# Five hand-overs of a streaming-encoder layer: output weights, residual sums, one split, the order of FFN up's last products, and places and order of FFN down's first tiles

## The chip, the cores and the metric

The kernel runs on one core of one Trainium2 chip. The metric is the device time of one execution in microseconds (us), less is better. The engines are named as the profile names them: PE multiplies matrices (PEld is its weight load), DVE, ACT and POOL do elementwise work, SP issues most of the DMA transfers. Three runs of the kernel before are given, and one execution of it with a profile.

## What is computed

One layer of a streaming encoder over 1024 tokens of width 1024, in float32. Cut to what matters here:

```
mod = silu(c) @ ada_w + ada_b                       # six vectors: sh1, sc1, g1, sh2, sc2, g2
h = rmsnorm(x, ln1_g) * (1 + sc1) + sh1
q, k, v, cb, cc, cx, ga, gb = split(h @ w_in)
y_a = stick_breaking_attention(rmsnorm(q), rmsnorm(k), v)
y_b = cb * causal_dwconv(cc * cx, conv_w)
merged = sigmoid(ga) * (y_a @ w_branch_a) + sigmoid(gb) * (y_b @ w_branch_b)
x = x + g1 * (merged @ w_out)
h = rmsnorm(x, ln2_g) * (1 + sc2) + sh2
f = (silu(h @ w_ffn_gate) * (h @ w_ffn_up)) @ w_ffn_down      # hidden width 2816
x = x + g2 * f
```

## The kernel before

**Products.** Each float32 operand is split into a high part, which is a copy rounded to the PE's type (`whi`, `rh`), and a low part, the rest (`wlo`, `rl`). A product of two operands is three matmuls: high by high, high by low, low by high (L131 to L133, in `half_prod`; L1596 to L1598 in FFN down). A `split` makes the two parts of 512 columns of weights: ACT copies (`whi`, L1227), and DVE subtracts (`wlo`, L1228). So a weight goes from DMA to ACT to DVE to PE, and PE can take `whi` one step earlier than `wlo`.

**Stages and their times on the time axis of the profile.** Input projection and attention run to about 968 us. The branch projection (loop at L1174) multiplies by `w_a` and merges the branches, up to 1068. The output projection (loops at L1311) goes over two halves `ch` of the 1024 output columns, and within a half over eight token tiles `i`; it ends at 1163. FFN gate and up (`strassen`, loop over `j` = 0 to 10 at L1520) run to 1586, FFN down (`down`) to 1803. In a program with one instruction list per engine, each engine works through its own list in order; a scheduler orders the lists when the kernel is built, from the order of the code, and `tc.issue_after(x)` holds what is issued under it behind `x`. A tile with `bufs=1` has one buffer: whoever writes it next waits until the last reader is done.

**Output weights.** `preload_wo` (L1145) loads five blocks of 512 columns of `w_o` in three DMAs (`raw`, two of 1024 columns and one of 512) and splits them. It is called from the `w_a` loop two rows of `m` before the loop's end (L1175), ahead of the load of that row's `w_a`. Its three loads share one buffer of their own pool `wpx`.

**Residual sums.** After each tile's product `ps`, DVE multiplies it by `g1b` into `tm` (L1356, one buffer) and adds the residual `xi`. In the first half of the columns the sum goes into `tm` and is stored to `d_x1` (L1358, L1359); in the second half it goes into the right half of `x1` (L1363, two buffers), whose left half is loaded back. From `x1` ACT makes `xn` (L1373), the normed tile, which PE transposes later (`tail_tr`, L1251) into `h2b`, FFN's input.

**FFN gate and up.** `strassen` computes 2 x 2 blocks of columns and tokens with seven products instead of eight. The factors made of token blocks are `rh[q]`, `rl[q]` (q = 0 to 6), those made of weight blocks are sums `s1` to `s4` that are split when they are used. The products lie in PSUM banks, which the trace names `e`. The end of one call is, in order: p1 takes another product onto itself (`prod(p1, split(s1), 4, True)`); ACT copies p1 into `c12`; PE computes p3; DVE adds p7 to the copy (`c22`); then p7 takes a product onto itself. The program lines say this order; the scheduler may put PE's products in another one. `hidden` multiplies up by gate for each of the four results, and `put_f` stores seven tiles f (high and low part, 128 x 1024) to `d_f[q, j]`; for the last `j` the stores go through POOL's queue. For j = 0 the products are written out by hand ahead of the loop (L1393 to L1447): `split_big` makes `rh[4]`, `rl[4]` from the input, `up2 = split(ws1[1])` splits a sum of weights.

**FFN down.** `down` runs seven products q in the order 0, 1, 2, 5, 4, 6, 3, each over 11 blocks j of the hidden width and four token tiles; 12 matmuls per block and 132 per product. The weights `w_d` lie in four buffers `wd` that held FFN's inputs and in six more (`wdx`); the stored f tiles come back through a ring of six buffers, with f `q`,`j` loaded by `get_f`. All of this is allocated in the pool `phe2`, which takes the place of the pools of FFN up (`phe`, with `rh6`, `rl6`, `rh3`, `rl3`): a tile there waits for the last reader of what lay at the same place. The allocation order before:

```
u2t = [e2.tile([P, 512], F32, name=f"u2t{t}") for t in range(4)]
vt = [e2.tile([P, 512], F32, name=f"vt{t}") for t in range(4)]
f0 = e2.tile([P, 2, 512], F32R, tag="f", bufs=6, name=nm("f"))
```

SP issues, per block, the load of the weights and then the load of f (L1582 to L1585), so the first f stands behind those weight loads whose place comes free late.

## Time and profile before

| What | Value |
| --- | --- |
| three runs | 1808.14, 1805.36, 1806.92 us |
| their median | 1806.92 us |
| the profiled execution | 1806.53 us, of which the span from the first to the last instruction is 1804.5 |
| mean granted clock of PE | 0.997 of full speed |
| DMA | 359.07 MB, 199 GB/s over the span |

Each profile row below has the start in the span (us), the duration (us), the engine (SPq and POOLq are the queues that issue DMAs), the program line, the operation, the result and the operands with their shape. Brackets at the end give the idle time of the engine just before the row, and who ended it. The names are the program's, without buffer numbers; several buffers share one name. A row of the waits view has the engine, the tile and the line that waited, after the arrow who ended the wait, and then the waits' total, their number and the longest, in us. A row of the windows view has the stretch (from and to, us from the span's start), its length, the busy times of PE, PEld, DVE, ACT and POOL with their counts of instructions, then PE's granted clock, the busy share of the DMA engines, and GB/s. A row of the DMA view ends with the median time from issue to landing, or is headed by its least, median and most.

Matmuls overlap, so that a row's duration is longer than the distance to the next one's start; the distance is what counts for the time.

### The profile page before, as it was taken

The page shows a single profiled execution, that of the slowest core. Times are in us where ns is not written, and L with a number is a line of the kernel's source. Part 1 is how long each engine was busy: PE and PEld are TensorE (multiplying, and loading weights), DVE is VectorE, ACT ScalarE, POOL GpSimd, SP SyncE. Part 2 cuts the span into 40 slices and gives each one's busy share as a digit, 9 for nine tenths or more (in the row PEclk, how much of TensorE's full clock was granted, in tenths as well). Part 3 has the DMA queues.
Part 4 walks back from the last instruction along what each step waited for, and adds up shares of the span by engine and source line. Part 5 has one row for each costly group of instructions (what it writes and reads, how often), then busy time and mean ns, then how long its engine had stood idle before and what let it go on. Part 6 is the DMA issues. An engine that isn't in the chain of part 4 may idle for free.

```text
span 1804.5 us, 24915 instructions
## 1 busy us (share of the span) xinstructions
PE 1785.0 (99%) x8599; PEld 1486.4 (82%) x8599; DVE 1271.7 (70%) x2030; ACT 829.8 (46%) x1553; POOL 343.0 (19%) x437
## 2 busy tenths in 40 slices
PE   8999999999999999999999999999999999999999
PEld 6888877888888888888888888888888888878887
DVE  6876586777774678777785764698777777544776
ACT  5534364333433567766675221764544454432321
POOL 0024334723231333333341100100000000000000
PEclk9999999999999999999999999999999999999999
DMA  9569654223644967796655856425534344389776
GB/s 377 165 239 383 237 186 141 88 94 101 224 137 155 289 187 197 218 321 169 165 141 191 281 193 200 139 94 181 192 129 162 139 178 163 129 325 319 276 232 223
DMA packets 165009, 359.07 MB, mean 199 GB/s; under 512 B 15538, under 2 KB 60938, under 8 KB 163732
## 3 DMA queue, kind: packets, MB, share of 16 engines
q1 hardware_dynamic: 128300, 289.65, 48.9%
q10 hardware_dynamic: 33096, 55.25, 8.5%
q0 software_dynamic: 3488, 12.59, 2.0%
q8 instruction: 68, 1.11, 0.3%
q14 instruction: 57, 0.47, 0.1%
HBM read 247.84 MB, written 109.62 MB: 198 GB/s over the span
## 4 chain that ended last, share of the span: by engine, by line
PE 88%; DMA 4%; DVE 3%; ACT 2%; issue 1%; POOL 1%; ACTq 0%; SPq 0%; DVEq 0%; POOLq 0%
PE pj L293 9%; PE e L133 7%; PE e L131 7%; PE e L132 7%; PE pj L133 6%; PE pj L131 6%; PE pj L132 6%; PE pj L1018 4%; PE pj L1020 4%; PE pj L1019 4%; PE e L1596 4%; PE e L1598 4%; PE e L1597 4%; PE tr L942 3%; PE o L958 2%; PE z L913 2%
## 5 line engine op out<-in xcount | busy, mean ns | idle before, releaser
L1227 ACT ACTIVATE whi<-raw 128x512 fp32r<-128x512 f32 x137 | 84.9, 628 | 159.9 <-PE e L132 99.9
L136 POOL TENSOR_TENSOR pt<-pt 128x63 f32<-128x63 f32 (+7 forms) x128 | 101.8, 795 | 212.0 <-DVE pt L928 195.7
L1228 DVE TENSOR_TENSOR wlo<-raw,whi 128x512 fp32r<-128x512 f32 x137 | 93.2, 687 | 67.3 <-ACT whi L1227 49.8
L293 PE MATMUL pj<-whi,big 128*128 128x512 f32 x448 | 133.7, 396 | 3.8 <-ACT big L262 3.8
L132 PE MATMUL e<-big,whi 128*128 128x512 f32 x352 | 137.0, 389 | 0.0
L133 PE MATMUL e<-big,wlo 128*128 128x512 f32 x352 | 136.3, 389 | 0.6 <-DVE wlo L1228 0.6
L131 PE MATMUL e<-big,whi 128*128 128x512 f32 x352 | 136.5, 390 | 0.0
L946 DVE TENSOR_TENSOR atl<-tr,ath 128x512 fp32r<-128x512 f32 (+1 forms) x192 | 104.1, 553 | 34.2 <-ACT ath L945 32.9
L136 DVE TENSOR_TENSOR c<-pj,c 128x512 f32<-128x512 f32 x140 | 93.5, 683 | 47.3 <-PE pj L133 46.8
L131 PE MATMUL pj<-big,whi 128*128 128x512 f32 x320 | 125.0, 391 | 0.0
L133 PE MATMUL pj<-big,wlo 128*128 128x512 f32 x320 | 124.8, 390 | 0.0
L1596 PE MATMUL e<-whi,f 128*128 128x512 f32 (+1 forms) x319 | 122.5, 384 | 2.3 <-DMA f<-d_f 2.3
L132 PE MATMUL pj<-big,whi 128*128 128x512 f32 x320 | 124.6, 389 | 0.0
L1597 PE MATMUL e<-wlo,f 128*128 128x512 f32 (+1 forms) x319 | 122.3, 384 | 0.0
L1598 PE MATMUL e<-whi,f 128*128 128x512 f32 (+1 forms) x319 | 122.3, 384 | 0.0
L915 ACT ACTIVATE pt<-z,rq 128x128 f32<-128x128 f32 (+1 forms) x192 | 107.3, 579 | 26.7 <-PE z L914 23.7
L1018 PE MATMUL pj<-big,whi 128*128 128x512 f32 x256 | 113.2, 442 | 0.0
L136 DVE TENSOR_TENSOR wlo<-raw,whi 128x512 fp32r<-128x512 f32 x108 | 88.6, 824 | 29.8 <-ACT whi L516 29.6
L945 ACT ACTIVATE ath<-tr 128x512 fp32r<-128x512 f32 (+1 forms) x192 | 93.3, 488 | 28.7 <-PE tr L942 27.5
L131 PE MATMUL e<-rh,whi 128*128 128x512 f32 x264 | 102.8, 389 | 1.4 <-DVE c L136 1.4
L293 PEld LDWEIGHTS pj<-whi,big 128*128 128x128 f32 x448 | 84.8, 190 | 22.3 <-ACT big L262 4.6
L132 PE MATMUL e<-rl,whi 128*128 128x512 f32 x264 | 102.7, 389 | 0.0
(300 smaller groups left out, 4736.7 us busy)
## 6 DMA issues: line engine op xcount, KB each, us to landing
f<-d_f SPq DMA_DIRECT2D x77, 512.0 KB, 4.7
d_f<-fs SPq DMA_DIRECT2D x70, 512.0 KB, 3.2
raw<-w_cg SPq DMA_DIRECT2D x40, 512.0 KB, 3.6
raw<-w_u SPq DMA_DIRECT2D x26, 512.0 KB, 4.3
raw<-w_g SPq DMA_DIRECT2D x25, 512.0 KB, 4.0
raw<-w_kv SPq DMA_DIRECT2D x20, 512.0 KB, 5.0
ld<-ada SPq DMA_DIRECT2D x16, 512.0 KB, 6.8
d_t<-ts SPq DMA_DIRECT2D x16, 512.0 KB, 6.5
```

What stands on the lines that cost most here:

```text
L131: nc.tensor.matmul(ps, wh[:, k, :], fh[:, k, :], start=(k == 0 and not onto), stop=False, skip_group_check=onto)
L132: nc.tensor.matmul(ps, wh[:, k, :], fl[:, k, :], start=False, stop=False, skip_group_check=onto)
L133: nc.tensor.matmul(ps, wl[:, k, :], fh[:, k, :], start=False, stop=(k == 3), skip_group_check=onto)
L136: eng.tensor_tensor(out=out, in0=a, in1=b, op=op)
L293: nc.tensor.matmul(ps, a, b, start=(k == 0 and q == 0), stop=(k == KT - 1 and q == 2))
L915: nc.scalar.activation(pt[:, off + s0:off + s0 + m], z[:, :m], AF.Sigmoid, scale=rq[:, 1, i, h:h + 1])
L945: nc.scalar.activation(th[:, :nb, c0:c0 + P], src, AF.Copy)
L946: nc.vector.tensor_tensor(out=tl[:, :nb, c0:c0 + P], in0=src, in1=th[:, :nb, c0:c0 + P].bitcast(F32), op=ALU.subtract)
L1018: nc.tensor.matmul(ps, wh, rh_, start=(k == 0), stop=False)
L1596: nc.tensor.matmul(o, sh, w[0][:, c], start=(j == 0), stop=False)
L1597: nc.tensor.matmul(o, sh, w[1][:, c], start=False, stop=False)
L1598: nc.tensor.matmul(o, sl, w[0][:, c], start=False, stop=(j == NJ - 1))
```

## The change

Five places are edited.

- **Output weights:** `preload_wo` is called one row of `m` later, and after that row's load of `w_a`. Its first two loads use the ring `raw` of the weight pool `gw`, the third has a tile of 512 columns of its own in `wpx`.
- **Residual sums:** in the second half of the columns the product with `g1b` goes directly into `x1`, and the residual is added there; `tm` is used in the first half only.
- **One split:** `up2 = split(ws1[1])` stands ahead of the `split_big` of `rh[4]`.
- **FFN up's last products:** in the last call (j = 10, up) p3 is held behind the last matmul of the product onto p1. For this `prod` and `half_prod` return that matmul.
- **FFN down's first tiles:** the six f buffers have a name each, and are allocated as f4, f5, then two of the `wdx`, then f0 to f3; `rh3`, `rl3` are now allocated before `rh6`, `rl6`. The loads of f 0 to f 6 stand before those of the weights, and the weight loads from the ninth on are held behind the load of f 1.

```diff
@@ half_prod, prod
-            nc.tensor.matmul(ps, wl[:, k, :], fh[:, k, :], start=False, stop=(k == 3), skip_group_check=onto)
+            last = nc.tensor.matmul(ps, wl[:, k, :], fh[:, k, :], start=False, stop=(k == 3), skip_group_check=onto)
+        return last
...
-        half_prod(ps, w, rh[q], rl[q], onto)
+        return half_prod(ps, w, rh[q], rl[q], onto)
@@ preload_wo
-            raw = wx.tile([P, 1024], F32, tag="raw", bufs=1, name=nm("raw"))
+            raw = wx.tile([P, 512], F32, name=nm("raw")) if j == 2 else gw.tile([P, 1024], F32, tag="raw", bufs=GR, name=nm("raw"))
@@ the w_a loop
+        if n == 0:
+            wa[m] = load_ch(w_a[m])
+        if (m, n) == (KT - 1, 0):
             with tc.issue_after(last_m.ins):
                 preload_wo()
-        if n == 0:
-            wa[m] = load_ch(w_a[m])
@@ residual sums
-            tm = dp.tile([P, 512], F32, tag="tm", bufs=1, name=nm("tm"))
-            nc.vector.tensor_tensor(out=tm, in0=ps, in1=g1b[:, cs], op=ALU.mult)
             if ch == 0:
+                tm = dp.tile([P, 512], F32, tag="tm", bufs=1, name=nm("tm"))
+                nc.vector.tensor_tensor(out=tm, in0=ps, in1=g1b[:, cs], op=ALU.mult)
...
-            nc.vector.tensor_tensor(out=x1[:, cs], in0=tm, in1=xi, op=ALU.add)
+            nc.vector.tensor_tensor(out=x1[:, cs], in0=ps, in1=g1b[:, cs], op=ALU.mult)
+            nc.vector.tensor_tensor(out=x1[:, cs], in0=x1[:, cs], in1=xi, op=ALU.add)
@@ ahead of the FFN loop
-    for q in (6, 3):
+    for q in (3, 6):
         rh[q] = ep.tile([P, 4, 512], F32R, name=f"rh{q}")
         rl[q] = ep.tile([P, 4, 512], F32R, name=f"rl{q}")
...
+    up2 = split(ws1[1])
     split_big(rh[4], rl[4], h2b[0][1])
-    up2 = split(ws1[1])
@@ strassen
-            prod(p1, split(s1), 4, True)
+            last5 = prod(p1, split(s1), 4, True)
...
-        p3 = product(sp_4 or split(s4), 2)
+        with tc.issue_after(last5.ins) if (j, e) == (NJ - 1, 1) else ExitStack():
+            p3 = product(sp_4 or split(s4), 2)
@@ ahead of down
-    f0 = e2.tile([P, 2, 512], F32R, tag="f", bufs=6, name=nm("f"))
+
+    def f_tile(n):
+        return e2.tile([P, 2, 512], F32R, tag=f"f{n % 6}", bufs=1, name=nm("f"))
+
+    fring = {n: f_tile(n) for n in (4, 5)}
+    wdx = [e2.tile([P, 1024], F32, name=nm("wdx")) for n in range(2)]
+    fring.update((n, f_tile(n)) for n in range(4))
+    nf = itertools.count()
     wd = [bigp.tile([P, 4, 1024], F32, tag="big", bufs=4, name=nm("wd")) for n in range(4)]
-    wd = [w_[:, n, :] for w_ in wd for n in range(4)] + [e2.tile([P, 1024], F32, name=nm("wdx")) for n in range(2 * NJ - 16)]
+    wd = [w_[:, n, :] for w_ in wd for n in range(4)] + wdx
+    wd += [e2.tile([P, 1024], F32, name=nm("wdx")) for n in range(2 * NJ - 18)]
+
     def get_f(q, j):
-        f = e2.tile([P, 2, 512], F32R, tag="f", bufs=6, name=nm("f")) if (q, j) != (0, 0) else f0
+        n = next(nf)
+        f = fring.pop(n) if n in fring else f_tile(n)
...
+    for ht in range(7):
+        ftiles[0, ht] = get_f(0, ht)
+        if ht == 1:
+            f1_ld = last_f[0]
     for ht in range(NJ):
-        load_wd(ht, 0)
-        if ht < 7:
-            ftiles[0, ht] = get_f(0, ht)
+        with tc.issue_after(f1_ld.ins) if ht > 7 else ExitStack():
+            load_wd(ht, 0)
```

How the change moves instructions shows at three places. The rows give the line, the operation and the tiles with the numbers that the build gave them; the waits name what an instruction waits for (DMAHW, DMASW: transfers that were issued by hardware or software queues; PE, Activation, DVE, Pool: instructions of these engines), and what an engine has waited for already is not waited for again.

**SP at the start of FFN down, before.** `wd` is a buffer of four weight blocks, `f_15660` is f 0, `f_15674` f 1.

```order
L1580 DMA wd_15662<-w_d 128x512 [waits DMAHW1_49,PE_49]
L1580 DMA wd_15662<-w_d 128x512 [waits DMAHW2_49]
L1580 DMA wd_15662<-w_d 128x512 [waits DMAHW3_49]
L1580 DMA wd_15662<-w_d 128x512 [waits DMAHW4_49]
L1580 DMA wd_15663<-w_d 128x512 [waits DMAHW5_49,PE_49]
L1580 DMA wd_15663<-w_d 128x512 [waits DMAHW6_49]
L1580 DMA wd_15663<-w_d 128x512 [waits DMAHW7_49]
L1571 DMA f_15660<-d_f_0_12410 128x1024 [waits DMAHW0_49]
L1571 DMA f_15674<-d_f_1_12411 128x1024 [waits DMAHW1_49,PE_49]
L1571 DMA f_15677<-d_f_2_12412 128x1024 [waits DMAHW2_49,Pool_49]
```

The same place after the change, where `f_15656` is f 0, and `f_15652` and `f_15653` are f 4 and f 5; `wd_15661` is the buffer that was `wd_15662`.

```order
L1594 DMA wd_15661<-w_d 128x512 [waits DMAHW4_49]
L1585 DMA f_15656<-d_f_0_12402 128x1024 [waits DMAHW5_49,PE_49,Pool_49]
L1585 DMA f_15657<-d_f_1_12403 128x1024 [waits DMAHW6_49]
L1585 DMA f_15658<-d_f_2_12404 128x1024 [waits DMAHW7_49]
L1585 DMA f_15659<-d_f_3_12405 128x1024 [waits DMAHW0_49,Pool_49]
L1585 DMA f_15652<-d_f_4_12406 128x1024 [waits DMAHW1_49,PE_49]
L1585 DMA f_15653<-d_f_5_12407 128x1024 [waits DMAHW2_49]
L1594 DMA wd_15662<-w_d 128x512 [waits DMAHW3_49]
L1594 DMA wd_15662<-w_d 128x512 [waits DMAHW4_49]
L1594 DMA wd_15662<-w_d 128x512 [waits DMAHW5_49]
```

The six loads f 0 to f 5 moved ahead of the last three weight loads. The load of f 0 has taken over a wait for PE, the one of f 4 has a wait for PE of its own, and the weight loads behind it have none any more.

**PE at the end of FFN up, before.** Each product is twelve matmuls; the first three of it (one of four k) are shown, and then the first of the next. `e_15580` is p3, `e_15400` the gate's last product, `e_15481` p1, `e_15540` p7.

```order
L131 MATMUL e_15580<-rh_11566,whi_15576 128x512
L132 MATMUL e_15580<-rl_11567,whi_15576 128x512
L133 MATMUL e_15580<-rh_11566,wlo_15577 128x512
...
L131 MATMUL e_15400<-rh_12189,whi_15450 128x512
...
L131 MATMUL e_15481<-big_12185,whi_15554 128x512
L132 MATMUL e_15481<-big_12186,whi_15554 128x512
L133 MATMUL e_15481<-big_12185,wlo_15555 128x512
...
L131 MATMUL e_15540<-rh_12189,whi_15618 128x512
...
L1596 MATMUL e_15700<-whi_15704,f_15660 128x512
```

The same stretch after the change: `e_15392` is the gate's last product, `e_15473` p1, `e_15572` p3, `e_15532` p7.

```order
L131 MATMUL e_15392<-rh_12179,whi_15442 128x512
...
L131 MATMUL e_15473<-big_12177,whi_15546 128x512
L132 MATMUL e_15473<-big_12178,whi_15546 128x512
L133 MATMUL e_15473<-big_12177,wlo_15547 128x512
...
L131 MATMUL e_15572<-rh_11566,whi_15568 128x512
L132 MATMUL e_15572<-rl_11567,whi_15568 128x512
L133 MATMUL e_15572<-rh_11566,wlo_15569 128x512
...
L131 MATMUL e_15532<-rh_12179,whi_15610 128x512
...
L1613 MATMUL e_15692<-whi_15696,f_15656 128x512
```

The twelve matmuls of p3 moved from ahead of the gate's last product to between p1's and p7's last ones.

**DVE at the turn to the second half of the output columns, before.** The first row is the last sum of the first half; `e` is the product, `xr` the residual tile.

```order
L1358 TENSOR_TENSOR tm_11517<-tm_11517,xr_11490 128x512 [waits DMAHW0_49,DVE_49]
L1356 TENSOR_TENSOR tm_11602<-e_11577,g1b 128x512 [waits DMAHW5_49,DVE_49,PE_49]
L1363 TENSOR_TENSOR x_2259_11604<-tm_11602,xr_11575 128x512 [waits DMAHW2_49,DVE_49]
L1356 TENSOR_TENSOR tm_11643<-e_11618,g1b 128x512 [waits DVE_49,PE_49]
L1363 TENSOR_TENSOR x_2267_11645<-tm_11643,xr_11616 128x512 [waits DMAHW6_49,DVE_49]
L1356 TENSOR_TENSOR tm_11694<-e_11659,g1b 128x512 [waits DVE_49,PE_49]
L1363 TENSOR_TENSOR x_2277_11696<-tm_11694,xr_11657 128x512 [waits DMAHW0_49,DMAHW7_49,DVE_49,Activation_49]
```

The same seven rows after the change.

```order
L1360 TENSOR_TENSOR tm_11517<-tm_11517,xr_11490 128x512 [waits DMAHW0_49,DVE_49]
L1365 TENSOR_TENSOR x_2258_11602<-e_11577,g1b 128x512 [waits PE_49]
L1366 TENSOR_TENSOR x_2258_11602<-x_2258_11602,xr_11575 128x512 [waits DMAHW2_49,DVE_49]
L1365 TENSOR_TENSOR x_2265_11642<-e_11617,g1b 128x512 [waits PE_49]
L1366 TENSOR_TENSOR x_2265_11642<-x_2265_11642,xr_11615 128x512 [waits DMAHW6_49,DVE_49]
L1365 TENSOR_TENSOR x_2274_11692<-e_11657,g1b 128x512 [waits DMAHW7_49,PE_49,Activation_49]
L1366 TENSOR_TENSOR x_2274_11692<-x_2274_11692,xr_11655 128x512 [waits DMAHW0_49,DVE_49]
```

The first product of the second half no longer waits for a transfer; from the third on, the waits for the `x1` buffer (a transfer and ACT) moved from the sum to the product.

## The prediction
> **What bounds the kernel now.** I read the page's busy times first, then the waits of PE (who ended them, total us, times, longest), then the timeline around each wait.
>
> ```profile
> PE 1785.0 (99%) x8599; PEld 1486.4 (82%) x8599; DVE 1271.7 (70%) x2030; ACT 829.8 (46%) x1553; POOL 343.0 (19%) x437
> ...
> PE e L1596 <- DMA f<-d_f: 2.3, 1, 2.3
> PE e L131 <- DVE c L136: 1.4, 1, 1.4
> ...
> PE e L1251 <- ACT xn L1373: 0.9, 1, 0.9
> PE e L1346 <- ACT whi L1154: 0.6, 1, 0.6
> PE e L133 <- DVE wlo L1228: 0.6, 1, 0.6
> ```
>
> PE is busy for 99% of the span, so only its pauses can be won. These five lie behind attention, one at each of the five hand-overs that the change touches; together they are 5.8 us. A busy row overlaps the next matmul, so I price each pause by the distance from start to start. The undisturbed distance is in the first two rows here: by the order 36 matmuls lie between them, (1581.83 - 1573.67) / 36 = 0.2267 us.
>
> ```profile
> 1573.67 0.39 PE L133 MATMUL e<-rh,wlo 128*128 128x512 f32 x1
> ...
> 1581.83 0.39 PE L133 MATMUL e<-big,wlo 128*128 128x512 f32 x1
> 1583.63 0.50 PE L131 MATMUL e<-rh,whi 128*128 128x512 f32 x1 [1.41 <-DVE c L136]
> 1583.97 0.40 PE L132 MATMUL e<-rl,whi 128*128 128x512 f32 x1
> ...
> 1582.26 0.60 ACT L1500 ACTIVATE c<-e 128x512 f32<-128x512 f32 x1 [1.36 <-PE e L133]
> ...
> 1582.89 0.69 DVE L136 TENSOR_TENSOR c<-e,c 128x512 f32<-128x512 f32 x1 [2.66 <-ACT c L1500]
> ```
>
> **FFN up's last products.** The matmul at 1581.83 closes p1. ACT copies p1, DVE adds p7 to the copy, and only then may PE go on adding onto p7: 1.80 from start to start, 1.57 over the norm, and 0.11 over on the next distance (0.34). In the change the twelve matmuls of p3 lie between. On the old time axis p1 then closes 12 x 0.2267 = 2.72 earlier: copy at 1579.54, add at 1580.17, and PE is released 0.74 after the add's start, as now, at 1580.9. It comes to that point at 1582.06. The cover is p3 with 1.1 us to spare; without it 1.57 would come back. Saved: **1.68**.
>
> **FFN down's first tiles.**
>
> ```profile
> 1583.35 0.43 SPq L1571 DMA_DIRECT2D f<-d_f  x1
> ...
> 1586.26 0.39 PE L133 MATMUL e<-rh,wlo 128*128 128x512 f32 x1
> 1588.98 0.47 PE L1596 MATMUL e<-whi,f 128*128 128x512 f32 x1 [2.33 <-DMA f<-d_f]
> ...
> 1589.91 0.63 PE L1596 MATMUL e<-whi,f 128*128 128x512 f32 x1
> ...
> 1592.47 0.63 PE L1596 MATMUL e<-whi,f 128*128 128x512 f32 x1
> ...
> 1591.00:1593.00 2.00, 2.00 (x6) 1.51 (x6) 2.00 (x4) 0.00 (x0) 0.53 (x1) 0.51 1.01 389
> ...
> DMA to landing us min/median/max: 4.8/5.9/7.9
> ```
>
> f 0 goes out at 1583.35, after three w_d loads that wait on SP for p1's operands, and lands 5.6 later: 2.72 between starts, 2.49 over, and 0.08 on the next distance. Then some 8 distances are 0.427 (six of them from 1589.91 to 1592.47), each 0.2 over: the granted clock of the windows row is 0.51. That costs **1.53** (by the timeline 0.16, five to six of 0.2, 0.19). In the change SP issues f 0 to f 3 ahead of those three loads. By the sizes in the code they begin 32 KB into the new pool, 18 KB past the 14 KB of sums, in rh6 and rl6 (rh3 and rl3 are the 16 KB before), whose last reader is the matmul at 1573.67. So f 0 can go at 1574.06 and, at the slowest f load of this stretch (7.9, the last row), lands at 1582.0. PE comes to FFN down 13 distances after 1581.83, at 1584.78. f 4 and f 5 still wait for the last product, but are needed 48 x 0.2267 = 10.9 after it; behind them on SP stand three w_d loads that are needed after 96 matmuls. Saved: **2.57**, and, as no pause is left to slow the clock, the 1.53.
>
> The half clock here follows pauses of 1.41 and 2.33, each under 3 us. [...]
>
> **Output weights.**
>
> ```profile
> 1055.05 0.53 POOL L649 DMA_DIRECT2D d_g<-mrow  x1 [14.54 <-ACT mrow L648]
> ...
> 1068.05 0.33 SPq L1150 DMA_DIRECT2D raw<-w_o  x1
> ...
> 1073.43 0.63 ACT L1154 ACTIVATE whi<-raw 128x512 fp32r<-128x512 f32 x1 [6.21 <-DMA raw<-w_o]
> ...
> 1073.12 0.39 PE L1346 MATMUL e<-whi,big 128*128 128x512 f32 x1
> 1074.11 0.50 PE L1346 MATMUL e<-whi,big 128*128 128x512 f32 x1 [0.60 <-ACT whi L1154]
> 1074.44 0.39 PE L1347 MATMUL e<-wlo,big 128*128 128x512 f32 x1
> ...
> d_g<-mrow POOLq DMA_DIRECT2D x1, 4.0 KB, 3.5
> ```
>
> Three loads share one buffer, so the third goes out at 1068.05, lands 5.4 later and costs PE 0.76, and 0.10 on the next distance: **0.86**. In the change two loads use the ring of w_a, and only the third needs a place that POOL's store of d_g frees. That wait is new. Its store starts at 1055.58 and lands by 1059.1 (3.5, the last row) or, if it took as long as the slowest load above, by 1063.5. With 5.4 for the load and 1.4 for its two halves the weights stand at 1065.9 or 1070.3. PE starts this stage 21 distances before 1073.12, at 1068.4, and wants them 12 later, at 1071.1. Nothing at both ends; a gain is excluded, for before has no such wait. Queued behind it are the last gate load on SP and some copies and splits on ACT and DVE; PE wants those for the fifth token tile, over 20 us later.
>
> **Residual sums.**
>
> ```profile
> 1125.37 0.69 DVE L1356 TENSOR_TENSOR tm<-e,g1b 128x512 f32<-128x512 f32 x1 [5.67 <-DMA d_x<-tm]
> ...
> 1129.33 1.15 ACT L1373 ACTIVATE xn<-x,rs_r 128x1024 f32<-128x1024 f32 x1 [0.97 <-POOL rs_r L123]
> ...
> 1129.25 0.39 PE L1348 MATMUL e<-whi,big 128*128 128x512 f32 x1
> 1130.53 1.09 PE L1251 MATMUL e<-dm,xn 128*128 128x128 f32 x8 [0.89 <-ACT xn L1373]
> ```
>
> The second half's first product waits at DVE for the store that still reads tm's one buffer. By the order 41 matmuls follow it up to 1129.25, so it is complete near 1129.25 - 41 x 0.2267 + 0.39 = 1120.3. Written straight into x1, its sum can start there, 5 us earlier, and xn, 4 us after the sum as now, is there near 1125.4. Even 3 us of waiting for the x tile would not reach PE. Saved: 1.28 - 0.23 = **1.05**. The new wait, for the x1 of two tiles before, costs nothing: that tile's xn ends with the transposes still ahead of it, at least one product (24 x 0.2267 = 5.4) before.
>
> **One split.**
>
> ```profile
> 1187.67 2.35 DVE L136 TENSOR_TENSOR big<-h2b,big 128x1024 fp32r<-128x1024 f32 x2
> 1189.94 0.68 DVE L1228 TENSOR_TENSOR wlo<-ws,whi 128x512 fp32r<-128x512 f32 x1
> ...
> 1189.74 0.39 PE L132 MATMUL e<-big,whi 128*128 128x512 f32 x1
> 1190.68 0.50 PE L133 MATMUL e<-big,wlo 128*128 128x512 f32 x1 [0.55 <-DVE wlo L1228]
> 1191.01 0.40 PE L131 MATMUL e<-big,whi 128*128 128x512 f32 x1
> ```
>
> The change puts this wlo ahead of the pair at 1187.67, so it ends at 1188.4 instead of 1190.6; the pair ends 0.6 later, and is read 12 matmuls further on. PE comes 0.86 + 1.05 = 1.91 earlier, at 1188.06. If DVE's chain stayed where it is, 0.3 of wait would be left; it starts at the sum that moves up by 5 us, so I count none. Saved: 0.71 + 0.10 = **0.81**.
>
> **Sum.** 1.68 + 2.57 + 1.53 + 0.86 + 1.05 + 0.81 = 8.50. The profiled execution took 1806.53 (span 1804.5 and 2.0 around it), so the forecast is 1806.53 - 8.5 = **1798.0**. The median of the three runs, 1806.92, is 0.4 higher, and they spread from 1805.36 to 1808.14. A difference of 0.2% (3.6 us) is about what a measurement can tell from no change here.
>
> **Rivals.**
>
> ```profile
> 1608.73 0.32 SPq L1647 DMA_DIRECT2D g2b<-d_g  x1
> ...
> 1616.18 0.63 ACT L1227 ACTIVATE whi<-wd 128x512 fp32r<-128x512 f32 x1 [10.10 <-DMA wd<-w_d]
> ...
> 1616.84 0.69 DVE L1228 TENSOR_TENSOR wlo<-wd,whi 128x512 fp32r<-128x512 f32 x1 [9.80 <-ACT whi L1227]
> ```
>
> *The wait moves to FFN down's second product.* Its weights come behind g2b on SP, and g2b waits for POOL's last stores of the hidden state; wlo ends at 1617.5. PE now comes there 132 x 0.2267 = 29.9 after 1584.78, at 1614.7. If those stores do not move, PE waits 2.6, and a new half-clock window could add 1.5: 1800.6 to 1802.1. For it: nothing in the change touches the stores. Against it: their chain starts with the copy of p1, which moves up by 2.72, just enough, and 2 MB of f loads leave their stretch. Chance 0.17.
>
> *The chain on ACT and DVE does not move up* and only PE comes earlier: the 1.91 of the two early hand-overs is lost again ahead of 1190, 1799.9. Against it stands the 5.67 at the head of that chain. Chance 0.09.
>
> *The clock falls all the same*: 1799.5, the 1.53 kept. Against it: the other pauses of this part of the span, all under 1 us, had none, and the dip stands right behind the two longest. Chance 0.08. [...]
>
> *f 0 lies elsewhere than I count* and waits for the last product. Then it goes out at 1584.9 and lands 4.8 to 7.9 later. The pause would be 4.9 to 8.0 instead of 2.49, and a second half-clock window adds 1.5. Against the 4.4 saved in the four other places: from 1806.1 (4.9, and 1.5 more) to 1809.2, slower than before once the load takes about 5.3. It would also mean that the change does not do what it says. Against it: its wait on POOL, which in that region only earlier tiles can have, fits my count of places. Chance 0.06, half of it slower, a third of that by over 0.2%.
>
> **How the numbers follow.** Forecast 0.60, rivals 0.17, 0.09, 0.08 and 0.06. The range starts 2.2 below the forecast (1.8, the spread below the median and a little more, and the 0.4 of the median) and reaches over the first three rivals to 1802.1, and 1.2 further (from the median to the highest run), to 1803.3; the fourth and sums of rivals are left out. Faster by over 0.2% (under 1803.3): the forecast and the first three rivals less 0.04 for their sums, 0.90; same 0.08; slower 0.02.
>
> **What would show it.** In the profile of the changed kernel the five waits quoted first should be gone from the waits of PE; f 0 should go out about 10 us before its first matmul; the granted clock should be 1.00 at the start of FFN down; the first sum of the second half should not wait for a store. A wait of PE for wlo or wd some 30 us into FFN down would be the first rival, a wait for a split or xn near the old 1165 to 1190 the second. I would be wrong altogether if f 0 still waited for the last product, or if POOL's store of d_g took over 9 us.

## The result and the profile after

| Kernel | Median (lowest to highest), us | Profiled execution, us (span) |
| --- | --- | --- |
| before | 1806.24 (1805.36 to 1808.14), 4 runs | 1806.53 (1804.5) |
| changed | 1797.19 (1795.54 to 1797.36), 4 runs | 1797.03 (1795.0) |

The ratio is 0.9946, 95% interval 0.9929 to 0.9964. In a later comparison of the same two kernels (the last experiment below) it was 0.9966, 0.9953 to 0.9979: 1797.64 beside 1803.48. The intervals overlap; the changed kernel came out alike both times, and the kernel before 2.8 lower. Two executions of the kernel before in the later comparisons, of 1876.93 and 4634.34 us, lie far outside all others and are left out of the ratios.

The waits of PE in the changed kernel, all rows (who waited, for whom, total us, times, longest):

```profile
PE tr L943 <- POOL pt L137: 2.8, 2, 2.4
PE pj L294 <- ACT big L263: 2.7, 1, 2.7
PE tr L325 <- POOL mk L90: 2.5, 1, 2.5
PE o L958 <- ACT ath L946: 0.9, 1, 0.9
PE pj L258 <- ACT vs L310: 0.6, 1, 0.6
```

The five rows of the tile `e` are gone; what is left lies in and before attention. Now the timeline of the changed kernel at the end of FFN up (start, duration, engine and line, result and operands, idle time before):

```profile
1570.54 11.64 SPq L1585 DMA_DIRECT2D f<-d_f  x6
...
1575.53 0.39 PE L133 MATMUL e<-big,wlo 128*128 128x512 f32 x1
...
1575.95 0.60 ACT L1503 ACTIVATE c<-e 128x512 f32<-128x512 f32 x1 [1.36 <-PE e L133]
...
1576.58 0.69 DVE L137 TENSOR_TENSOR c<-e,c 128x512 f32<-128x512 f32 x1 [2.66 <-ACT c L1503]
...
1578.24 0.39 PE L133 MATMUL e<-rh,wlo 128*128 128x512 f32 x1
...
1580.96 0.39 PE L133 MATMUL e<-rh,wlo 128*128 128x512 f32 x1
1581.19 0.39 PE L1613 MATMUL e<-whi,f 128*128 128x512 f32 x1
```

p1 closes at 1575.53, p3 at 1578.24, p7 at 1580.96, and FFN down follows at the plain distance of 0.23. DVE's add starts at 1576.58. In the trace of before PE went on with p7 0.74 after the add's start (1582.89 to 1583.63); by that estimate it could have done so here at 1577.32, and it comes to p7 at 1578.47: p3 covers the hand-over with 1.15 to spare. The first of the six f loads went out at 1570.54, 10.65 before its first matmul.

The clock, in a window of the changed kernel at the start of FFN down (stretch, length, busy times of PE, PEld, DVE, ACT, POOL, granted clock, DMA share, GB/s):

```profile
1581.00:1583.00 2.00, 2.00 (x10) 1.66 (x9) 2.00 (x4) 0.64 (x1) 0.00 (x0) 1.00 0.32 68
```

The half clock is gone too. The other hand-overs of the changed kernel, from the timeline:

```profile
1054.71 0.53 POOL L650 DMA_DIRECT2D d_g<-mrow  x1 [14.17 <-ACT mrow L649]
1057.80 0.33 SPq L1151 DMA_DIRECT2D raw<-w_o  x1
1061.98 0.69 DVE L1156 TENSOR_TENSOR wlo<-raw,whi 128x512 fp32r<-128x512 f32 x1 [0.94 <-ACT whi L1155]
...
1118.77 0.69 DVE L1365 TENSOR_TENSOR x<-e,g1b 128x512 f32<-128x512 f32 x1 [3.71 <-PE e L1350]
1122.71 1.16 ACT L1376 ACTIVATE xn<-x,rs_r 128x1024 f32<-128x1024 f32 x1 [0.97 <-POOL rs_r L123]
1127.86 1.03 PE L1253 MATMUL e<-dm,xn 128*128 128x128 f32 x8
...
1183.62 0.68 DVE L1230 TENSOR_TENSOR wlo<-ws,whi 128x512 fp32r<-128x512 f32 x1
1187.25 0.39 PE L133 MATMUL e<-big,wlo 128*128 128x512 f32 x1
...
1609.97 0.69 DVE L1230 TENSOR_TENSOR wlo<-wd,whi 128x512 fp32r<-128x512 f32 x1 [8.90 <-ACT whi L1229]
1611.34 0.39 PE L1614 MATMUL e<-wlo,f 128*128 128x512 f32 x1
```

The third load of output weights does wait for the store of d_g (from 1054.71 to 1057.80) and is split by 1062.67. The first sum of the second half waits for PE and for no store, xn is ready 4.0 before PE's transposes, the wlo of the moved split 2.95 before PE. Closest of these is FFN down's second product: its first wlo ends at 1610.66, and PE takes it at 1611.34, 0.68 later.

Where the time went, by the last matmul (1800.61 before, 1791.08 after: 9.53):

| Stretch | us |
| --- | --- |
| up to the last pause in attention (its matmul starts at 977.78, 977.44) | 0.34 |
| the five places and the half clock, as priced in the prediction | 8.50 |
| the same places beyond their price (half clock 1.60 for 1.53, `xn` 1.10 for 1.05) | 0.12 |
| a sixth pause, at the turn to the second half of the columns | 0.34 |
| spread thinly over the rest, not located | 0.23 |

In the trace of before attention's last matmul starts at 980.99; the list of stages has it end at about 968.

The sixth is hidden in a row that joins two matmuls. The timeline of before:

```profile
1115.95 1.15 ACT L1227 ACTIVATE whi<-raw 128x512 fp32r<-128x512 f32 x2 [21.39 <-DVE tm L1358]
...
1116.17 0.96 PE L1346 MATMUL e<-whi,big 128*128 128x512 f32 x2
```

The same two matmuls in the timeline of the changed kernel:

```profile
1114.94 0.62 PE L1348 MATMUL e<-whi,big 128*128 128x512 f32 x2
```

In the changed kernel the two take 0.62 together; before, the second started 0.23 later than that and the next one another 0.11, while ACT was splitting the weights of the second half. A joined row hides a pause.

### The profile page after: what moved, and what is told of

The parts are those of the page before. It is cut to its first block, busy times and chain, and to the rows that moved or that the text cites. A ratio compares the mean times of both kernels' runs of the same rounds, so it can differ in the third digit from the quotient of the medians.

```text
span 1795.0 us, 24911 instructions
## 1 busy us (share of the span) xinstructions
PE 1781.7 (99%) x8599; PEld 1485.0 (83%) x8599; DVE 1270.1 (71%) x2030; ACT 829.6 (46%) x1553; POOL 343.3 (19%) x437
## 4 chain that ended last, share of the span: by engine, by line
PE 96%; DMA 2%; ACT 1%; DVE 0%; issue 0%; POOL 0%; SPq 0%; POOLq 0%; DVEq 0%; ACTq 0%
PE e L132 8%; PE e L133 8%; PE e L131 8%; PE pj L131 7%; PE pj L133 7%; PE pj L132 7%; PE pj L294 7%; PE pj L1019 5%; PE pj L1020 5%; PE pj L1021 5%; PE e L1613 4%; PE e L1614 4%; PE e L1615 4%; PE tr L943 3%; PE o L959 2%; PE z L914 2%
## 5 line engine op out<-in xcount | busy, mean ns | idle before, releaser
L137 DVE TENSOR_TENSOR c<-pj,c 128x512 f32<-128x512 f32 x140 | 93.4, 683 | 47.6 <-PE pj L133 47.0
```

The source lines that it names most:

```text
L137: eng.tensor_tensor(out=out, in0=a, in1=b, op=op)
```

## The experiments

Twelve kernels ran, eleven with some parts of the change undone and one with none, four on one chip at a time beside the kernel before. The last three columns are of the one traced execution of each, behind attention alone. "Pauses" are those of PE, from start to start, over the undisturbed 0.23. "Longer" is the time from the matmul behind attention's last pause to the kernel's last matmul, over that of the changed kernel (1791.08 - 977.44 = 813.64 us); in the kernel before it is 9.2.

| Undone | Median, us | Ratio to before (95%) | Pauses, us | Half clock | Longer |
| --- | --- | --- | --- | --- | --- |
| f tiles | 1799.65 | 0.9973 (0.9962, 0.9984) | 0.78, 0.15 | no | 1.3 |
| p3's order | 1798.94 | 0.9977 (0.9967, 0.9986) | 1.57, 0.11 | no | 1.9 |
| f tiles and p3's order | 1801.73 | 0.9991 (0.9980, 1.0001) | 1.57, 2.50 | 3.4 | 6.0 |
| order of rh3 and rh6 alone | 1802.62 | 0.9995 (0.9986, 1.0005) | 3.55 | 6.8 | 6.4 |
| SP's order alone | 1798.83 | 0.9977 (0.9966, 0.9988) | 1.84 | no | 2.0 |
| output weights | 1798.18 | 0.9972 (0.9961, 0.9983) | none | no | 0.1 |
| residual sums | 1797.10 | 0.9960 (0.9948, 0.9972) | none | no | 0.1 |
| split | 1795.51 | 0.9961 (0.9947, 0.9976) | none | no | 0.1 |
| these three together | 1799.60 | 0.9984 (0.9974, 0.9994) | 0.22, 1.00, 0.66 | no | 2.3 |
| sums and split | 1797.73 | 0.9968 (0.9957, 0.9979) | 0.33 | no | 0.6 |
| weights and split | 1797.99 | 0.9966 (0.9952, 0.9980) | 1.08, 1.19 | no | 2.6 |
| nothing | 1797.64 | 0.9966 (0.9953, 0.9979) | none | no | 0.1 |

The kernel before took 1800.72 to 1807.65 in the 28 executions beside the first four, so a single time says little about 1 us; the pauses in the traces do, but of one execution each. The ratios are those on record for all executions; the quotients of the medians differ from them by up to 0.0009.

### FFN's end

**The f tiles' places and order undone.**

```diff
-    for q in (3, 6):
+    for q in (6, 3):
...
-    fring = {n: f_tile(n) for n in (4, 5)}
+    f0 = e2.tile([P, 2, 512], F32R, tag="f", bufs=6, name=nm("f"))
...
     for ht in range(NJ):
+        load_wd(ht, 0)
+        if ht < 7:
+            ftiles[0, ht] = get_f(0, ht)
```

> The changed kernel (1797.2 us beside 1806.2 of before) with the places and the order of FFN down's first tiles as before; the four other parts stay. Theory A (f 0's load stands on SP behind three w_d loads that wait for p1's last product, and only its landing counts): p1 now closes 12 matmuls earlier, so f 0 is sent about 4.1 before FFN down's first matmul is due and lands 5.6 later: PE waits about 1.5 there, not the 2.49 of before. If the granted clock needs both pauses of before (1.41 and 2.33 close together) to fall, it stays at 1.0 and the time is about 1798.7. Theory B (one pause above 1 us is enough for the half clock): a stretch of half clock follows, 1.5 more, about 1800.2. Rival (the part is worth what the trace of before showed, 2.57 and 1.53, whatever the other parts do): about 1801.3.

The timeline of this kernel:

```profile
1575.46 1.28 SPq L1584 DMA_DIRECT2D wd<-w_d  x3
1576.78 6.60 SPq L1575 DMA_DIRECT2D f<-d_f  x6
...
1581.71 0.47 PE L1600 MATMUL e<-whi,f 128*128 128x512 f32 x1 [0.62 <-ACT whi L1229]
```

f 0 goes out at 1576.78, behind the three weight loads, and PE goes on 4.93 later. The row names ACT, but the splits of these first weights were long done (they start at 1576.18), so it was f 0. The pause is 0.78, half of what was expected, because the load took 4.9 and not 5.6; it is far from the 2.49 and 1.53 that the part was worth in the trace of before. With p1 closed earlier, most of that gain is there without this part in this execution. It is one of the shorter ones, with 1797.79: four of the seven took 1799.65 to 1800.12, and what they waited for was not traced.

**p3's order undone.**

```diff
-        with tc.issue_after(last5.ins) if (j, e) == (NJ - 1, 1) else ExitStack():
-            p3 = product(sp_4 or split(s4), 2)
+        p3 = product(sp_4 or split(s4), 2)
```

> The changed kernel with FFN up's last products in the order of before; the four other parts stay. Theory A: PE waits 1.57 to 1.68 for c22 behind p1 again; besides, the stores of the hidden state hang on the copy of p1, which comes 12 matmuls (2.72) later against the products ahead of it while FFN down starts only 1.68 later; in the changed kernel the second product's first wlo is ready 0.45 ahead of PE, so PE waits about 0.6 there: 1797.2 + 1.7 + 0.6 = 1799.5, with both waits in the trace. Rival (only the pause itself): 1798.9, and no wait at FFN down's second product. Clock: one pause of 1.41 alone; if that is enough for the half clock, 1.5 more and a granted clock near 0.5 for 3.4 us.

The timeline has the one pause, and FFN down's second product at its limit:

```profile
1579.53 0.50 PE L131 MATMUL e<-rh,whi 128*128 128x512 f32 x1 [1.41 <-DVE c L137]
...
1611.80 0.69 DVE L1230 TENSOR_TENSOR wlo<-wd,whi 128x512 fp32r<-128x512 f32 x1 [8.76 <-ACT whi L1229]
1612.54 0.50 PE L1613 MATMUL e<-wlo,f 128*128 128x512 f32 x1
```

wlo ends at 1612.49, and PE takes it at 1612.54, just late: 0.12 on this distance and the next, where 0.6 was expected. The expectation had counted the margin of the changed kernel to the product's first matmul (0.45); wlo is read by the second (0.68).

**Both undone.**

```diff
-    for q in (3, 6):
+    for q in (6, 3):
...
-        with tc.issue_after(last5.ins) if (j, e) == (NJ - 1, 1) else ExitStack():
+        p3 = product(sp_4 or split(s4), 2)
```

> The changed kernel with both parts of FFN's end undone (order of the last products, first tiles of FFN down); output weights, residual sums and the split stay. Theory A (the pauses of 1.57 and 2.49 and the half clock stand and fall with these two parts): the end of FFN up and the start of FFN down look as before, 5.8 over the changed kernel, about 1803.0, granted clock near 0.5 for 3.4 us behind the second pause. Rival (the half clock was chance or hangs on the time since an earlier event): the two pauses come back without it, about 1801.5.

The idle times in the timeline of this kernel:

```profile
1580.29 0.50 PE L131 MATMUL e<-rh,whi 128*128 128x512 f32 x1 [1.41 <-DVE c L137]
1585.65 0.47 PE L1599 MATMUL e<-whi,f 128*128 128x512 f32 x1 [2.34 <-DMA f<-d_f]
```

Both pauses and the half clock are back, as in before to 0.01. So 1.57, 2.50 and the half clock stand and fall with the two parts, though not each with one: together 5.9 (1.57, 2.50, 1.60 of half clock and 0.19 on the distances behind the pauses), apart 0.78 and 1.57 in pauses.

**rh6 and rl6 allocated first again.**

```diff
-    for q in (3, 6):
+    for q in (6, 3):
```

> The changed kernel with one edit: rh6, rl6 are allocated ahead of rh3, rl3 again, so that f 0 to f 3 lie on rh3 and rl3, which FFN up's last product reads. Theory A (the place decides): f 0 goes out when the last product has ended, about 0.2 after FFN down's first matmul is due, lands 4.8 to 7.9 later, and PE waits 5.0 to 8.1; 1802.2 to 1805.3, and if one long pause brings the half clock, 1.5 more. Rival (the order on SP decides, the place does not): no pause, about 1797.2.

The timeline of this kernel at the turn to FFN down:

```profile
1582.25 0.39 PE L133 MATMUL e<-rh,wlo 128*128 128x512 f32 x1
...
1582.70 2.75 SPq L1585 DMA_DIRECT2D f<-d_f  x6
...
1586.03 0.77 PE L1613 MATMUL e<-whi,f 128*128 128x512 f32 x1 [3.40 <-DMA f<-d_f]
```

f 0 goes out when the last product has ended, and PE waits 3.40: the place decides, and this one edit takes away nearly the whole gain (0.9995 of before; 6.4 us in the trace). The load landed within 3.33, so the pause was shorter than the 5.0 to 8.1 expected.

**SP's order undone, the places kept.**

```diff
-    for ht in range(7):
-        ftiles[0, ht] = get_f(0, ht)
...
     for ht in range(NJ):
-        with tc.issue_after(f1_ld.ins) if ht > 7 else ExitStack():
-            load_wd(ht, 0)
+        load_wd(ht, 0)
+        if ht < 7:
+            ftiles[0, ht] = get_f(0, ht)
```

> The changed kernel with the new places of the f tiles, but SP's order of before: f 0 behind the three w_d loads that wait for p1's last product. Theory A (the place frees the buffer, the order lets the load use it; neither is enough alone): f 0 goes out about 4.1 ahead of FFN down's first matmul and lands 5.6 later, PE waits about 1.5, as with places and order both undone: 1798.7 (1800.2 with a half clock). Rival (the place alone brings the gain): no pause, 1797.2.

The timeline at the same place:

```profile
1577.43 5.18 SPq L1585 DMA_DIRECT2D f<-d_f  x6
...
1583.37 0.47 PE L1610 MATMUL e<-whi,f 128*128 128x512 f32 x1 [1.68 <-DMA f<-d_f]
```

The place alone brings nothing: f 0 goes out as late before PE's time as with places and order undone (4.1), and PE goes on 5.94 after it. Place and order are needed together.

### The early hand-overs

**Output weights undone.**

```diff
-            raw = wx.tile([P, 512], F32, name=nm("raw")) if j == 2 else gw.tile([P, 1024], F32, tag="raw", bufs=GR, name=nm("raw"))
+            raw = wx.tile([P, 1024], F32, tag="raw", bufs=1, name=nm("raw"))
...
-        if (m, n) == (KT - 1, 0):
+        if (m, n) == (KT - 2, 0):
```

(The last line stands in one with the call ahead of the load of `w_a`, as in before.)

> The changed kernel with the preload of the output weights as before (call two rows ahead of the loop's end, one buffer). Theory A: PE waits 0.76 + 0.10 at the thirteenth matmul of the output projection again, nothing else changes: 1798.1. Rival (the wait was covered by slack further on): the pause is in the trace, and the time stays at 1797.2, with another pause shorter.

No pause. The third load stands behind the second's splits again, but was split 3.2 after its issue (1066.11, ACT at 1069.28), not 5.4.

**Residual sums undone.**

```diff
+            tm = dp.tile([P, 512], F32, tag="tm", bufs=1, name=nm("tm"))
+            nc.vector.tensor_tensor(out=tm, in0=ps, in1=g1b[:, cs], op=ALU.mult)
...
-            nc.vector.tensor_tensor(out=x1[:, cs], in0=ps, in1=g1b[:, cs], op=ALU.mult)
-            nc.vector.tensor_tensor(out=x1[:, cs], in0=x1[:, cs], in1=xi, op=ALU.add)
+            nc.vector.tensor_tensor(out=x1[:, cs], in0=tm, in1=xi, op=ALU.add)
```

> The changed kernel with the residual sums through tm as before. Theory A: DVE waits about 5 us for the store that reads tm, xn comes about 4 us later, PE waits 1.05 to 1.3 for it (1.28 between the starts in the trace of before, where PE came 0.86 later: up to 1.9 if the store does not move up with PE), and the split's place ahead of split_big then carries the next hand-over: 1798.2 to 1799.1, one pause. Rival (the sum through tm costs DVE time all along the second half): more than one pause.

The timeline of this kernel, from the first sum of the second half to the transposes:

```profile
1120.84 0.69 DVE L1358 TENSOR_TENSOR tm<-e,g1b 128x512 f32<-128x512 f32 x1 [5.80 <-DMA d_x<-tm]
1124.79 1.16 ACT L1375 ACTIVATE xn<-x,rs_r 128x1024 f32<-128x1024 f32 x1 [0.97 <-POOL rs_r L123]
1126.59 1.04 PE L1253 MATMUL e<-dm,xn 128*128 128x128 f32 x8
```

DVE waits 5.80 for the store, as before, and yet PE does not wait: xn ends at 1125.95, 0.64 before the transposes. The wait for the store was not what made the 1.05 by itself. Expected 1 to 1.9, measured nothing.

**The split undone.**

```diff
-    up2 = split(ws1[1])
     split_big(rh[4], rl[4], h2b[0][1])
+    up2 = split(ws1[1])
```

> The changed kernel with the split behind split_big again. Theory A (the residual sums already bring DVE's chain up by about 3.5 us against before, PE only by 2.7): this wlo ends near 1186.6 in the span, and PE comes for it at 1187.25: no pause, 1797.2; the split is not needed once the sums are early. Rival (each of the five parts carries its own pause, as the sum of the prediction has it): 0.81 more, 1798.0, with the wait for wlo back in the trace.

The last wlo ahead of PE's need in the timeline of this kernel:

```profile
1184.30 0.68 DVE L1230 TENSOR_TENSOR wlo<-ws,whi 128x512 fp32r<-128x512 f32 x1
```

No pause, as theory A has it: wlo ends at 1184.98, and PE takes it at 1185.68, 0.70 later.

**All three undone.** The three edits above together.

> The changed kernel with the three early parts undone together (output weights, residual sums, the split); the two parts at FFN's end stay. Theory A (the three pauses are one chain: a late third block of output weights holds up the first product and with it DVE's sums, then xn, then the wlo): if the third w_o load lands over about 4.6 after its issue, as the 5.4 in the trace of before, all three pauses come back, 0.86 + 1.05 to 1.13 + 0.81 = 2.8 over the changed kernel; if it lands in 3.2 as in the run with only the output weights undone, the first pause is missing, and the others are shorter or missing too. Rival (each pause stands on its own, as the prediction has it): xn and wlo waits come back whole, 1.9, whatever the load does.

The timeline of this kernel at the four places:

```profile
1070.13 0.63 ACT L1155 ACTIVATE whi<-raw 128x512 fp32r<-128x512 f32 x1 [4.33 <-DMA raw<-w_o]
...
1123.29 0.69 DVE L1357 TENSOR_TENSOR tm<-e,g1b 128x512 f32<-128x512 f32 x1 [5.61 <-DMA d_x<-tm]
...
1128.43 1.09 PE L1252 MATMUL e<-dm,xn 128*128 128x128 f32 x8 [0.84 <-ACT xn L1374]
...
1188.58 0.50 PE L133 MATMUL e<-big,wlo 128*128 128x512 f32 x1 [0.51 <-DVE wlo L1229]
```

xn's and wlo's pauses are back (1.00 and 0.66, with the distances behind them 1.83, the 1.9 of the rival), and so is the sixth pause at the turn to the second half (0.22), but not the first: the third load was split in time. So the first pause isn't what causes the others, and the part of the chain theory that hung on it falls. What differs from the run with only the sums undone is the time of DVE's chain of sums: the first sum of the second half starts 56.05 after the stage's first matmul (1123.29 - 1067.24) here, 57.01 in before, and 54.10 there.

**Only the output weights kept.** Sums and split undone.

> The changed kernel with residual sums and the split undone, the output weights early. Theory A (chain): DVE still waits about 5.8 for the store of tm, but the sums start early enough, xn is ready about 0.6 ahead of PE, and the wlo behind split_big about 0.3 to 0.6 ahead: no pause, time of the changed kernel. Rival (own pauses): 1.05 + 0.81 = 1.9 more.

Two rows of its timeline:

```profile
1120.47 0.69 DVE L1358 TENSOR_TENSOR tm<-e,g1b 128x512 f32<-128x512 f32 x1 [5.08 <-DMA d_x<-tm]
...
1611.35 0.50 PE L1613 MATMUL e<-wlo,f 128*128 128x512 f32 x1 [0.17 <-DVE wlo L1230]
```

No pause at xn or wlo: with the weights early, the sum through `tm` starts 52.79 after the stage's first matmul, early enough. The row at 1611.35 is the prediction's first rival, 0.33 over the undisturbed distance at FFN down's second product.

**Only the residual sums kept.** Output weights and split undone.

> The changed kernel with output weights and the split undone, the residual sums straight into x1. Theory A (chain): a wait for the third block of output weights up to 0.86, by how fast its load lands (none at 3.2, 0.86 at 5.4); no wait for xn; wlo ready near or ahead of PE, wait 0 to 0.2. Rival (own pauses): 0.86 + 0.81 = 1.7 more.

Two rows of its timeline:

```profile
1076.99 0.63 ACT L1155 ACTIVATE whi<-raw 128x512 fp32r<-128x512 f32 x1 [5.86 <-DMA raw<-w_o]
...
1123.61 0.69 DVE L1364 TENSOR_TENSOR x<-e,g1b 128x512 f32<-128x512 f32 x1 [1.72 <-PE e L1349]
```

The third block of output weights comes late here, and PE waits 1.19 for it (the other pause, 1.08, lies ahead of this stage, in the branch projection). The first sum waits for PE alone, and neither xn nor wlo is waited for. So in these traces xn's and wlo's pauses are gone with the early weights alone and with the direct sums alone. That the split alone takes away wlo's is not shown: no kernel ran with it and without the other two.

**The changed kernel again.** Nothing undone.

> The changed kernel itself once more, beside the three others on one chip. Both theories: 0.9946 of before within the noise of the runs (9 us less), no pause of PE behind attention, granted clock 1.0 there; where the chain theory holds, the two kernels above it differ from this one by less than 1 us.

No pause and no half clock behind attention. The gain is 5.8 and not 9, and the ratio lies just outside the first interval; what differs is the kernel before.

This trace has the last sum of the first half later than the first trace of the changed kernel:

```profile
1115.45 0.68 DVE L1359 TENSOR_TENSOR tm<-e,g1b 128x512 f32<-128x512 f32 x1
```

That is 47.6 after the stage's first matmul (1067.83). Over all traces this sum starts 44.4 to 47.6 after it in the ten with early weights, and 45.7 to 48.9 in the four with late ones: the weights move the chain of sums, but the spread between executions is as large. Through `tm` the next sum starts 7.6 to 8.3 later (four traces), and with PE undelayed it may start 54.7 after the stage's first matmul at the latest (54.10 and the 0.64 to spare of the run with only the sums undone). By this limit, moved by the earlier pauses of PE, the two kernels that waited for xn should have waited 1.0 and 1.1; they waited 1.00 and 1.05. An estimate from these numbers: in three of the ten traces with early weights (47.0 to 47.6) a sum through `tm` would have come at 54.6 to 55.9, and PE would have waited up to 1.2. So early weights alone make xn's pause rarer, without ruling it out. Written directly, the first sum of the second half starts at 50.8 in nine of ten traces and at 52.1 in the other, when PE has finished its product, however late the chain is.

## Why the prediction was right, and where it was not

The time, 1797.19, lies 0.8 under the forecast of 1798.0. In the profiled execution each term of the sum was found with its size to within 0.07, and no new wait took its place; another 0.34 each came from attention and from the sixth pause, which the forecast did not have. The reasons behind them did less well.

- **FFN up's last products (1.68).** Right, spare time included: 1.1 forecast, 1.15 measured. Undone alone it costs 1.57 and 0.11 on the next distance, as priced, and 0.12 more at FFN down's second product.
- **FFN down's first tiles (2.57) and the half clock (1.53).** Right in sum: with p3's order undone too, 2.50 and the half clock come back (1.60, as in before, where seven distances are 0.2 over and not five to six). The step that failed is their independence of the term before: with p3 in place f 0 is sent 4.1 ahead of PE's time even in the old order, and the part undone alone costs 0.78 (1.84 with the places kept), with no half clock. Undone alone, the two parts cost 0.8 to 1.8 and 1.57 in pauses; undone together 5.9.
- **The clock.** The prediction had the half clock follow the pair of pauses. In the run with `rh6` first, one pause of 3.55 came with 6.82 of half clock; what counts in a pause for the clock was not shown (rows in the last section). The rival that the clock falls all the same is out: none of the eleven traces whose pauses at this place are 1.84 or less has it.
- **Output weights (0.86).** A wait of 0, 0, 0.76 and 1.19 in the four traces with the old preload. The term is a matter of when the third load goes out and how fast it lands: it was split 3.2, 3.5, 5.4 and 5.0 after its issue, which is 2.2, 2.9, 5.1 and 5.5 after the stage's first matmul. One trace could not tell that. In the ten traces with the new preload PE never waits there.
- **Residual sums (1.05) and split (0.81).** The step that failed is "its sum can start there, 5 us earlier", taken as worth 1.05 by itself, and 0.81 for the split beside it. The sum does start earlier, but undone alone neither edit cost anything in its trace (0.1 behind attention), since the chain of sums was early enough without it. Undone together with the output weights, the two pauses are back with 1.83. The prediction added terms that are in part alternatives. The sum came right because the change makes all of them.
- **The rivals.** The wait at FFN down's second product came with 0.33 in a kernel with sums and split undone, and with 0.12 where p3's order was; in the changed kernel the margin is 0.68, near the "just enough" of the prediction. The chain on ACT and DVE did move up: `xn` and wlo have 4.0 and 2.95 to spare. f 0 in a place that the last product reads is what the run with `rh6` first shows: 0.9995 of before, not the 1806.1 to 1809.2 beside 1806.5, since its load landed in 3.3, where the prediction took 4.8 to 7.9 from other loads.
- **The base.** The forecast started from one execution at 1806.53, and that it met the time is in part luck. Beside the experiments the medians of the kernel before were 1803.5 to 1804.1; from 1803.5 the same 8.5 would have led to 1795.0, where 1797.64 was measured. The executions of before differ, and the granted clock of each is on record: of the 70 beside the experiments, 16 with a mean of 0.999 took 1801.6 on average, 37 with 0.998 took 1803.7, 10 with 0.997 (the value of the traced one) 1805.3, and 7 with 0.996 1807.5. One stretch at half clock as long as the 3.41 us in the trace of before is 0.001 of the mean (3.41 x 0.5 / 1804); by this estimate some executions hold more such stretches than others. The traced one is not typical: 9 of the 70 took longer. In the nine executions of the changed kernel the mean is 0.998 or 0.999. Where the stretches lie in the untraced executions is not known. The experiments used three chips, and which one the first comparison used is not on record; its four executions of before took 1805.36 or more, as 17 of the 70 did. So what makes the 2.8 between the two comparisons stays open.

## What to carry to other kernels

Pauses in one trace add up to what was lost there, not to what each edit is worth: where two hand-overs hang on the same chain, one edit can remove both (here the 1.83 of xn and wlo, gone with the early weights alone and with the direct sums alone), and the second one then buys only a margin, which a later execution may need. And one trace is one execution: the same old preload cost between 0 and 1.19 in four. Undo each edit alone and in groups before keeping or crediting it. The f tiles that are loaded early needed both a place whose last reader is early and a spot in their queue ahead of what waits: with p3's order in place PE waited 1.84 with the place alone, 3.55 with the order alone, 0.78 with neither, and not at all with both.

## What the runs showed of the hardware

In the trace of before the granted clock at the start of FFN down was 0.50 for 3.41 us and 1.00 on both sides. Two windows of that length, the second of them the half clock (stretch, length, PE busy, granted clock, DMA share, GB/s):

```profile
1586.13:1589.55 3.42, 1.09 (x6) 1.00 0.77 270
1589.55:1592.96 3.41, 3.41 (x10) 0.50 1.04 390
```

The same view of the kernel with both FFN parts undone, in attention and at FFN down:

```profile
600.70:604.11 3.41, 1.50 (x8) 1.00 1.17 222
604.11:607.53 3.42, 2.94 (x16) 1.00 1.12 316
1583.74:1587.15 3.41, 1.50 (x7) 1.00 0.90 312
1587.15:1590.56 3.41, 3.41 (x10) 0.50 0.84 287
```

And of the kernel with p3's order undone, at the same place in attention:

```profile
598.55:601.96 3.41, 2.25 (x12) 1.00 1.16 225
601.96:605.37 3.41, 1.83 (x9) 1.00 1.17 263
```

And of the kernel with `rh6` first, at FFN down and in attention:

```profile
1581.61:1585.03 3.42, 1.03 (x5) 1.00 0.39 127
1585.03:1588.44 3.41, 2.41 (x6) 0.50 0.83 293
1588.44:1591.85 3.41, 3.41 (x10) 0.50 1.01 351
1591.85:1595.26 3.41, 3.41 (x17) 1.00 1.02 417
...
601.99:605.40 3.41, 1.06 (x7) 1.00 1.16 229
605.40:608.81 3.41, 3.41 (x13) 0.50 0.98 338
```

In these rows the windows at full clock with 1.03, 1.06 and 1.09 busy were each followed by half clock. Of the two with 1.50, the one at FFN down was followed by half clock, the one in attention by a window at 1.00. With p3's order undone PE was busy for 2.25 and then 1.83 of two windows on end, idle for 2.74 of the two together, and both are at 1.00, as is the one behind them (605.37 to 608.79). With SP's order undone the window from 1580.42 to 1583.83, in which PE waits 1.68 for f 0, has 1.73 busy, and the next one is at 1.00 too. These are single executions, and what makes the clock change they do not show.
